# A hybrid decoder layer on one core: the FFN norm's factors in the gate and up weights, sums in order of use, rows two tiles ahead

## The chip, the cores and the metric

The kernel runs on one core of one Trainium2 chip. Its time is the device time of one execution in microseconds (us); the figure compared is the median over runs. One core has TensorE (PE; its weight loads are listed apart as PEld), VectorE (DVE), ScalarE (ACT), GpSimd (POOL) and SyncE (SP), which here issues nearly all DMAs. Each engine works through its own instructions in a fixed order and waits on semaphores for the others.

## The reference

One decoder layer on `x` of 1024 rows and 1024 columns, all in float32. What matters here is its second half:

```python
x = x + rmsnorm(m @ w_out[i], mix_post_norm[i])
h = rmsnorm(x, ffn_pre_norm[i])
f = (jax.nn.silu(h @ w_gate[i]) * (h @ w_up[i])) @ w_down[i]
x = x + rmsnorm(f, ffn_post_norm[i])
...
def rmsnorm(x, g):
    y = xf * lax.rsqrt(jnp.mean(xf * xf, axis=-1, keepdims=True) + EPS)
    return (y * g.astype(jnp.float32)).astype(x.dtype)
```

`m` holds the normalised outputs of an attention group and of a convolution group, 512 columns each. The FFN is 2816 wide (`w_gate` and `w_up` are 1024 x 2816).

## The kernel before

**Arithmetic.** TensorE multiplies in a rounded form (fp32r). To keep float32 accuracy, `split` makes of each value a high half (a cast on ScalarE, L196) and a low half (a subtraction, L197, on VectorE in the stretch of interest); a product is then three matmuls: high by high, high by low, low by high.

**Stages.** Attention and convolution come first. The output projection is done in two halves: `wo_c` handles the convolution's columns and stores its result to `y_d`; `wo_a(t)`, for the eight row tiles t of 128 rows, loads that result and the rows of `x`, adds the attention's half (24 wide matmuls; L1003 adds the bank to `y`), takes the mean square (L217 on ScalarE), the power -0.5 (L213 on VectorE, L214 on GpSimd), multiplies by `mix_post_norm` (L1009), adds the rows of `x` (L1010; on GpSimd for the tiles in `XP`, that is 2, 4 and 6, else on VectorE), stores the new `x`, takes the mean square again, and makes the normalised row `n1` in one VectorE instruction that multiplies by the row's factor and by `ffn_pre_norm`, broadcast over partitions (L1016). `h2_turn(t)` transposes `n1` (L1037, eight transposes), copies the banks (L1039 for tiles 0 to 3, which are stored to `hr_d` at L1047; L1041 for 4 to 7, which stay) and splits them into `B11`, `B21`, `B22`.

**The FFN** is a seven-product scheme for a two-by-two block product (Strassen's, in Winograd's form). Two blocks of 128 FFN columns form a pair `fp`; there are 11 pairs, each with `m` = 0 (gate) and 1 (up). Products run in the order `ORDER`, (1, 2, 6, 5, 7, 3, 4), each of 12 wide matmuls (128x128 by 128x512; L1122, L1124, L1125). Its left operand comes from the weights: `raw_load(fp, i)` loads two raw tiles of 128x1024 (L1079), `factor(fp, m, p)` makes sums of their halves on GpSimd (L1092, L1093, L1098, L1101) and splits them. Its right operand is a block of the activations for products 1, 2, 3 and a block sum for 6, 5, 7, 4, called `T2`, `T1`, `T3`, `T4`. The sums of 128x2048 elements are L1205 and L1206 on VectorE and L1207 and L1215 on GpSimd. A product's bank is evacuated by a ScalarE copy (L1134) or a VectorE addition (L1140 and its neighbours L1138 and L1144); silu is L1142. `s_factors` stores sums of the result to `sc_d`, `w_factors` those of `w_down` to `wc_d`, for the down products (L1280 to L1282), which follow.

**What sets the order.** The source's order is an input to a scheduler at build time, which fixes each engine's instruction order. So the order on an engine can differ from the source's. Memory is managed by hand: `mf(n)` takes the least recently freed n units of 128x512 float32 (30 units in all), `mr(n)` those in fp32r (72 units), and a transfer into a buffer waits for the last reader of what lay there. The main loop over `seq` writes a factor five products ahead of its use (`AHEAD`).

Of the kernel before, what the change touches and what calls it, by code (L numbers as in the profile page):

```python
# [15 lines left out]
P = 128  # L16
# [116 lines left out]
def hybrid_layer(ctx: ExitStack, tc: tile.TileContext, x, x_t, p_t, cols_in, positions,  # L133
                 w_in, w_conv, q_norm, kv_norm, w_uq, w_ukv, w_out, mix_post_norm, ffn_pre_norm, w_gate, w_up, w_down, ffn_post_norm,
# [91 lines left out]
    rows = mem_rows.a[0:28, 0:P]  # L226
# [174 lines left out]
    wcol = cols(28)  # L401

    def columns():
# [3 lines left out]
        pe.transpose(b[:, 32:60], rows, ident[0:28, 0:28])  # L407
        dve.tensor_copy(posc, b[:, 0:T])
        dve.tensor_copy(wcol, b[:, 32:60])
# [584 lines left out]
    g_mix, g_ffn = mf(2, MG), mf(2, MG)  # L994
    brow(mix_post_norm, D, g_mix)
    brow(ffn_pre_norm, D, g_ffn)

    def wo_a(t):
        xr, y = mf(2, ML), mf(2, ML)
        sp.dma_start(xr.a, x[t * P : (t + 1) * P, :])  # L1000
        sp.dma_start(y.a, y_d[t * P : (t + 1) * P, :])
# [8 lines left out]
        (pool if t in XP else dve).tensor_tensor(y.a, y.a, xr.a, op=ALU.add)  # L1010
# [5 lines left out]
        dve.scalar_tensor_tensor(n1.a, y.a, r, g_ffn.a, op0=ALU.mult, op1=ALU.mult)  # L1016
# [63 lines left out]

    def factor(fp, m, p):
        a = raws[fp, m, 0].a
# [5 lines left out]
        else:  # L1088
            b = raws[fp, m, 1].a
            a21, a22 = b[:, 0:U], b[:, U:]  # L1090
            if p == 6:
                pool.tensor_tensor(a21, a21, a22, op=ALU.add)  # L1092
                pool.tensor_tensor(a11, a21, a11, op=ALU.subtract)  # L1093
                src = a11
            elif p == 5:
                src = a21
            elif p == 7:
                pool.tensor_tensor(a21, a22, a11, op=ALU.subtract)  # L1098
                src = a21
            elif p == 3:  # L1100
                pool.tensor_tensor(a12, a12, a11, op=ALU.subtract)  # L1101
                src = a12
            else:
                src = a22
# [73 lines left out]

    raw_load(0, 0, MW)
    for p in (1, 2):  # L1180
        for m in range(2):
            factor(0, m, p)
    tr[0], tr[1] = mf(4, ((22, 26),)), mf(4, ((26, 30),))
    for t in range(T):
        wo_a(t)
        if t > 0:
            h2_turn(t - 1)
    for d in (mTa, wo):
        for h, l in d.values():
            free(h, l)  # L1190
    free(g_mix, g_ffn)
    head = [(0, m, p) for p in (1, 2) for m in range(2)]
    raw_load(1, 0, MW)
    for i in head[:2]:
        product(*i)
    h2_turn(T - 1)
    b11 = mf(4, MG)
    sp.dma_start(four(b11), hr_d[:, 0:4, :])
    for i in head[2:]:
        product(*i)  # L1200
    for p in (1, 2):
        for m in range(2):
            factor(1, m, p)
    b12, b22 = tr[0], tr[1]
    dve.tensor_tensor(b12.a, b22.a, b12.a, op=ALU.subtract)  # L1205
    dve.tensor_tensor(b11.a, b12.a, b11.a, op=ALU.add)  # L1206
    pool.tensor_tensor(b22.a, b22.a, b11.a, op=ALU.subtract)  # L1207
    for n, v in (("T2", b11), ("T1", b22), ("T3", b12)):
        h, l = tf[n] = pair(4, BT)
        split(h.a, l.a, v.a)  # L1210
        if n != "T2":
            free(v)
# [3 lines left out]
    h, l = tf["T4"] = pair(4, BT)  # L1216
    split(h.a, l.a, b21.a)
    free(b11, b21)
    for p in (1, 2):
        for m in range(2):  # L1220
            product(1, m, p)
    raw_load(0, 1)
# [4 lines left out]
    for i in range(-AHEAD, len(seq)):  # L1227
        if i + AHEAD < len(seq):
            fp, m, p = seq[i + AHEAD]
            if p == 6 and m == 0:  # L1230
                if fp > 0:
                    raw_load(fp, 1)
            factor(fp, m, p)
            if p == 7 and m == 1 and 1 < fp + 1 < NP:
                raw_load(fp + 1, 0)
        if i >= 0:
            fp, m, p = seq[i]
            product(fp, m, p)
            if p == 5 and m == 1:
                w_factors(fp)  # L1240
            if p == ORDER[-1] and m == 1:
                s_factors(fp)
# [142 lines left out]
    for t in range(T - 3, T):  # L1385
# [4 lines left out]
        "w_ukv", "w_out", "mix_post_norm", "ffn_pre_norm", "w_gate", "w_up", "w_down",  # L1390
# [42 lines left out]
```

## Time and profile before

| | us |
|---|---|
| median of 3 runs | 1263.94 (1262.7 to 1264.12) |
| the profiled execution | 1265.35 |
| its span in the trace | 1263.6 |

Times in the views are counted from the start of the span. The page gives each engine's busy time, and in 40 slices its busy share in tenths. The views of the trace used below are: windows (busy time of each engine in a stretch), groups of instructions (by line and shape: count, busy time, mean duration in ns, idle time before and its releasers), TensorE's waits (who was waited for: us in total, times, longest) and the chain that ended last (start, length, what). An instruction is named by its line in the kernel, so L1003 is the addition in `wo_a`.

### The profile page before, as it was taken

How to read it: one execution, taken by the hardware profiler on the slowest of the kernel's cores; microseconds unless marked ns; L12 is line 12 of the kernel's file. 1: busy time of each engine (PE TensorE's matmuls, PEld its weight loads, DVE VectorE, ACT ScalarE, POOL GpSimd, SP SyncE). 2: the span in 40 equal slices, each digit the busy share in tenths (PEclk: the TensorE clock that was granted, in tenths of full speed). 3: DMA queues.
4: the chain of work that ended last, by engine and by line, in shares of the span. 5: the costliest groups of instructions: out<-in, count | busy, mean ns of one | idle time of the engine just before them, and what ended most of it. 6: DMA issues, size and time to landing. Idle time of an engine off the chain costs nothing.

```text
span 1263.6 us, 16523 instructions
## 1 busy us (share of the span) xinstructions
PE 1214.1 (96%) x5950; PEld 1024.2 (81%) x5950; DVE 775.4 (61%) x1114; ACT 558.0 (44%) x1011; POOL 494.5 (39%) x372
## 2 busy tenths in 40 slices
PE   7999999999999997759999999999999999999998
PEld 6898888888999886548888888888887888888886
DVE  7945457388867576687564564756547554566632
ACT  6543323277766744543333343333335445454220
POOL 5523545236634222287965665766611000000100
PEclk9999999999999999879999999999999999999999
DMA  6422554994541746435644445544349766665331
GB/s 244 169 67 99 192 184 152 287 343 113 136 104 57 285 164 203 158 110 190 230 160 142 144 157 183 175 167 147 137 126 327 239 194 190 196 217 169 105 112 50
DMA packets 87789, 215.67 MB, mean 171 GB/s; under 512 B 8791, under 2 KB 17275, under 8 KB 86395
## 3 DMA queue, kind: packets, MB, share of 16 engines
q1 hardware_dynamic: 87648, 214.60, 51.3%
q8 instruction: 46, 0.75, 0.3%
q14 instruction: 37, 0.30, 0.1%
q10 hardware_dynamic: 58, 0.02, 0.0%
HBM read 143.28 MB, written 71.04 MB: 170 GB/s over the span
## 4 chain that ended last, share of the span: by engine, by line
PE 79%; DVE 8%; DMA 8%; ACT 2%; issue 2%; POOL 2%; SPq 0%; DVEq 0%; ACTq 0%; POOLq 0%
PE banks L1124 10%; PE banks L1125 10%; PE banks L1122 10%; PE banks L207 7%; PE banks L208 7%; PE banks L209 7%; PE banks L1280 5%; PE banks L1281 5%; PE banks L1282 5%; DVE mem_r L197 4%; PE banks L842 2%; DMA mem_f<-y_d 2%; PE banks L813 1%; PE banks L809 1%; PE banks L814 1%
## 5 line engine op out<-in xcount | busy, mean ns | idle before, releaser
L197 DVE TENSOR_TENSOR mem_r<-mem_f,mem_r 128x512 fp32r<-128x512 f32 (+2 forms) x353 | 345.7, 1005 | 215.0 <-ACT mem_r L196 203.5
L196 ACT CAST mem_r<-mem_f 128x512 fp32r<-128x512 f32 (+3 forms) x356 | 234.7, 686 | 389.8 <-PE banks L1124 159.5
L1122 PE MATMUL banks<-mem_r 128*128 128x512 f32 x616 | 243.8, 396 | 10.9 <-DVE mem_f L1003 7.0
L1124 PE MATMUL banks<-mem_r 128*128 128x512 f32 x616 | 243.8, 396 | 10.1 <-DVE mem_r L197 10.1
L207 PE MATMUL banks<-mem_r 128*128 128x512 f32 (+2 forms) x664 | 247.1, 377 | 4.0 <-DVE mem_f L1003 3.3
L208 PE MATMUL banks<-mem_r 128*128 128x512 f32 (+2 forms) x664 | 247.4, 373 | 1.9 <-POOL mem_r L197 1.9
L209 PE MATMUL banks<-mem_r 128*128 128x512 f32 (+2 forms) x664 | 246.6, 373 | 0.0
L1125 PE MATMUL banks<-mem_r 128*128 128x512 f32 x616 | 243.0, 395 | 0.0
L214 POOL TENSOR_TENSOR small<-small,mhalf 128x1 f32<-128x1 f32 (+2 forms) x42 | 34.7, 828 | 318.2 <-DVE small L213 315.6
L1122 PEld LDWEIGHTS banks<-mem_r 128*128 128x128 f32 x616 | 117.8, 191 | 37.1 <-issue 7.4
L1124 PEld LDWEIGHTS banks<-mem_r 128*128 128x128 f32 x616 | 118.1, 192 | 35.4 <-DVE mem_r L197 11.0
L207 PEld LDWEIGHTS banks<-mem_r 128*128 128x128 f32 x664 | 126.0, 191 | 25.6 <-DVE mem_f L1003 3.8
L208 PEld LDWEIGHTS banks<-mem_r 128*128 128x128 f32 x664 | 126.5, 190 | 22.5 <-POOL mem_r L197 2.1
L209 PEld LDWEIGHTS banks<-mem_r 128*128 128x128 f32 x664 | 126.4, 190 | 21.0
L1125 PEld LDWEIGHTS banks<-mem_r 128*128 128x128 f32 x616 | 118.0, 192 | 25.0
L1280 PE MATMUL banks<-mem_r 128*128 128x512 f32 x308 | 119.1, 390 | 1.6 <-ACT mem_r L196 1.6
L1281 PE MATMUL banks<-mem_r 128*128 128x512 f32 x308 | 119.8, 389 | 0.0
L1282 PE MATMUL banks<-mem_r 128*128 128x512 f32 x308 | 118.8, 389 | 0.0
L827 POOL TENSOR_TENSOR mem_f<-mem_f,stats 128x640 f32<-128x640 f32 (+5 forms) x64 | 72.6, 1148 | 92.3 <-DVE stats L826 46.5
L197 DVE TENSOR_TENSOR mem_r<-banks,mem_r 128x512 fp32r<-128x512 f32 (+3 forms) x134 | 79.8, 621 | 14.5 <-ACT mem_r L196 13.6
L1140 DVE TENSOR_TENSOR mem_f<-banks,mem_f 128x512 f32<-128x512 f32 x66 | 45.3, 688 | 68.2 <-PE banks L1125 68.1
L196 ACT CAST mem_r<-banks 128x512 fp32r<-128x512 f32 (+3 forms) x134 | 67.3, 545 | 27.0 <-PE banks L842 13.6
(172 smaller groups left out, 1644.7 us busy)
## 6 DMA issues: line engine op xcount, KB each, us to landing
sc_d<-mem_f SPq DMA_DIRECT2D x77, 256.0 KB, 3.1
mem_f<-sc_d SPq DMA_DIRECT2D x77, 256.0 KB, 2.7
mem_f<-in_w_up_dram SPq DMA_DIRECT2D x22, 512.0 KB, 4.2
mem_f<-in_w_gate_dram SPq DMA_DIRECT2D x22, 512.0 KB, 4.6
mem_f<-in_w_down_dram SPq DMA_DIRECT2D x22, 512.0 KB, 4.5
wc_d<-mem_f SPq DMA_DIRECT2D x22, 512.0 KB, 3.0
mem_f<-wc_d SPq DMA_DIRECT2D x44, 256.0 KB, 3.0
mem_f<-in_w_down_dram SPq DMA_DIRECT2D x33, 256.0 KB, 3.3
```

Source lines behind the costliest of these rows:

```text
L196: act.copy(h, src)
L197: (eng or dve).tensor_tensor(l, src, h.bitcast(F32), op=ALU.subtract)
L207: pe.matmul(o, wh, vh, start=i == 0, stop=False)
L208: pe.matmul(o, wh, vl, start=False, stop=False)
L209: pe.matmul(o, wl, vh, start=False, stop=i == n - 1)
L827: pool.tensor_tensor(pt.a[:, 0:n], pt.a[:, 0:n], sm.to_broadcast([P, n]), op=ALU.mult)
L1122: pe.matmul(b, wh.a[:, c], th[:, k], start=first and k == 0, stop=False, skip_group_check=True)
L1124: pe.matmul(b, wh.a[:, c], tl[:, k], start=False, stop=False, skip_group_check=True)
L1125: pe.matmul(b, wl.a[:, c], th[:, k], start=False, stop=k == 3, skip_group_check=True)
L1280: pe.matmul(b, ah.a[:, c], bh.a, start=first, stop=False, skip_group_check=True)
L1281: pe.matmul(b, ah.a[:, c], bl.a, start=False, stop=False, skip_group_check=True)
L1282: pe.matmul(b, al.a[:, c], bh.a, start=False, stop=last, skip_group_check=True)
```

## The change

Six edits:

1. `ffn_pre_norm` is no longer broadcast to a row tile. Its 1024 values come in as eight more columns (`wcol`, 28 to 36), 128 values along the partitions in each. `raw_gain` multiplies the raw weights by them in place, eight `act.mul` of 128x128 on each raw tile (L1090), called from `factor` for p = 1 and p = 6. The row keeps only its own factor, applied by `act.mul` of 128x1024 on ScalarE (L1021 in the new file) where L1016 was on VectorE.
2. The rows of `x` and `y` are loaded by `wo_rows`, called two tiles ahead, `y` first.
3. `XP` is gone: the addition of `x` is on VectorE for all tiles.
4. `factor` runs its sums for pair 0 on VectorE.
5. The block sums L1207 and L1215 move from GpSimd to VectorE (L1237, L1246), and sums, splits, factors and products are written in order of use.
6. `raw_load(fp + 1, 1)` is written behind the last factor of pair fp instead of ahead of product 6 of pair fp + 1, and the four head products are written ahead of the last turn.

```diff
-    g_mix, g_ffn = mf(2, MG), mf(2, MG)
+    g_mix = mf(2, MG)
     brow(mix_post_norm, D, g_mix)
-    brow(ffn_pre_norm, D, g_ffn)
+    xy = {}
+    def wo_rows(t):
+        xr, y = xy[t] = mf(2, ML), mf(2, ML)
+        sp.dma_start(y.a, y_d[t * P : (t + 1) * P, :])
+        sp.dma_start(xr.a, x[t * P : (t + 1) * P, :])
     def wo_a(t):
...
-        (pool if t in XP else dve).tensor_tensor(y.a, y.a, xr.a, op=ALU.add)
+        dve.tensor_tensor(y.a, y.a, xr.a, op=ALU.add)
...
-        dve.scalar_tensor_tensor(n1.a, y.a, r, g_ffn.a, op0=ALU.mult, op1=ALU.mult)
+        act.mul(n1.a, y.a, r)
...
+    def raw_gain(fp, m, i):
+        r = raws[fp, m, i].a
+        for k in range(KD):
+            c = slice(k * P, (k + 1) * P)
+            act.mul(r[:, c], r[:, c], wcol[:, 28 + k : 29 + k])
     def factor(fp, m, p):
+        eng = pool if fp else dve
+        if p in (1, 6):
+            raw_gain(fp, m, int(p == 6))
...
+    wo_rows(0)
+    wo_rows(1)
     raw_load(0, 0, MW)
-    for p in (1, 2):
-        for m in range(2):
-            factor(0, m, p)
     for t in range(T):
+        if t + 2 < T:
+            wo_rows(t + 2)
         wo_a(t)
         if t > 0:
             h2_turn(t - 1)
+        if t == T // 2:
+            for p in (1, 2):
+                for m in range(2):
+                    factor(0, m, p)
...
-    for p in (1, 2):
-        for m in range(2):
-            factor(1, m, p)
     dve.tensor_tensor(b12.a, b22.a, b12.a, op=ALU.subtract)
+    both(factor, 1, 1)
+    both(product, 1, 1)
     dve.tensor_tensor(b11.a, b12.a, b11.a, op=ALU.add)
-    pool.tensor_tensor(b22.a, b22.a, b11.a, op=ALU.subtract)
+    t_split("T2", b11)
+    both(factor, 1, 2)
+    both(product, 1, 2)
+    both(factor, 0, 6)
+    dve.tensor_tensor(b22.a, b22.a, b11.a, op=ALU.subtract)
+    t_split("T1", b22)
...
-    pool.tensor_tensor(b21.a, b21.a, b11.a, op=ALU.subtract)
+    both(factor, 0, 5)
+    t_split("T3", b12)
+    factor(0, 0, 7)
+    dve.tensor_tensor(b21.a, b21.a, b11.a, op=ALU.subtract)
+    t_split("T4", b21)
...
-    for i in range(-AHEAD, len(seq)):
+    for i in range(len(seq)):
...
-            if p == 6 and m == 0:
-                if fp > 0:
-                    raw_load(fp, 1)
             factor(fp, m, p)
+            if p == ORDER[-1] and m == 1 and fp + 1 < NP:
+                raw_load(fp + 1, 1)
```

Each place below is a run of one engine's instructions in its order, as line, operation, output and input, and shape, with a count where equal ones follow one another. The first is ScalarE's, at the start of the tile loop. L946 evacuates the projection's first half, L196 casts, L217 is the mean square. Before:

```order
L946 ACTIVATE mem_f<-banks,small 128x512 x3
L196 CAST mem_r<-mem_f 128x512 x3
L946 ACTIVATE mem_f<-banks,small 128x512 x2
L217 ACTIVATE mem_f,small<-mem_f 128x1024 x5
L1039 COPY mem_f<-banks 128x512
```

And now:

```order
L946 ACTIVATE mem_f<-banks,small 128x512 x2
L1090 ACTIVATE mem_f<-mem_f,small 128x128 x8
L196 CAST mem_r<-mem_f 128x512
L946 ACTIVATE mem_f<-banks,small 128x512
L196 CAST mem_r<-mem_f 128x512
L946 ACTIVATE mem_f<-banks,small 128x512 x2
L1090 ACTIVATE mem_f<-mem_f,small 128x128 x8
L196 CAST mem_r<-mem_f 128x512 x2
L217 ACTIVATE mem_f,small<-mem_f 128x1024 x2
L1021 ACTIVATE mem_f<-mem_f,small 128x1024
```

The gains of pair 0's two first raw tiles (L1090) stand between the last evacuations of `wo_c` and the first mean square, though the source writes them behind tile 4.

The second place is ScalarE's at the end of the tile loop, in front of the last tile's turn. L1134 evacuates a product's bank and L1142 is silu with the load of its table. Before:

```order
L1134 COPY mem_f<-banks 128x512 x2
L196 CAST mem_r<-mem_f 128x512 x4
L1142 ACT_TABLE_LOAD
L1142 ACTIVATE mem_f<-mem_f 128x512
L1041 COPY mem_f<-banks 128x4x128 x2
L196 CAST mem_r<-banks 128x4x128
L217 ACTIVATE mem_f,small<-mem_f 128x1024
L1134 COPY mem_f<-banks 128x512
```

And now, where L1156 is that silu:

```order
L217 ACTIVATE mem_f,small<-mem_f 128x1024
L1090 ACTIVATE mem_f<-mem_f,small 128x128 x8
L1021 ACTIVATE mem_f<-mem_f,small 128x1024
L217 ACTIVATE mem_f,small<-mem_f 128x1024
L1090 ACTIVATE mem_f<-mem_f,small 128x128 x8
L1156 ACT_TABLE_LOAD
L1156 ACTIVATE mem_f<-mem_f 128x512
L196 CAST mem_r<-mem_f 128x512
L1021 ACTIVATE mem_f<-mem_f,small 128x1024
L1090 ACTIVATE mem_f<-mem_f,small 128x128 x8
```

Three sets of gains now lie around the last rows' multiplication L1021, two of them ahead of it, with the table load between.

The third place is VectorE's behind the last turn. L1205 is the first block sum, L1206 the second, L1140 an evacuation, L197 a low half. Before:

```order
L1205 TENSOR_TENSOR mem_f<-mem_f 128x2048
L197 TENSOR_TENSOR mem_r<-banks,mem_r 128x4x128
L1206 TENSOR_TENSOR mem_f<-mem_f 128x2048
L1140 TENSOR_TENSOR mem_f<-banks,mem_f 128x512
L197 TENSOR_TENSOR mem_r<-mem_f,mem_r 128x2048
```

And now, where L1229, L1232 and L1237 are the sums, L1154 an evacuation, and L1106 and L1107 factors of pair 0:

```order
L1229 TENSOR_TENSOR mem_f<-mem_f 128x2048
L197 TENSOR_TENSOR mem_r<-banks,mem_r 128x4x128
L197 TENSOR_TENSOR mem_r<-mem_f,mem_r 128x512 x2
L1232 TENSOR_TENSOR mem_f<-mem_f 128x2048
L1106 TENSOR_TENSOR mem_f<-mem_f 128x512
L197 TENSOR_TENSOR mem_r<-mem_f,mem_r 128x2048
L1154 TENSOR_TENSOR mem_f<-banks,mem_f 128x512
L1237 TENSOR_TENSOR mem_f<-mem_f 128x2048
L1107 TENSOR_TENSOR mem_f<-mem_f 128x512
L197 TENSOR_TENSOR mem_r<-mem_f,mem_r 128x2048
```

VectorE now holds the third sum (L1237) and the factors of pair 0 (L1106, L1107), which GpSimd had.

More of the change, by code (lines that the diff above doesn't have):

```diff
@@ L400, in hybrid_layer @@
     posc = cols(T)
-    wcol = cols(28)
+    wcol = cols(36)
     def columns():
@@ L406, in columns @@
         pe.transpose(b[:, 0:T], prow, ident[0:T, 0:T])
-        pe.transpose(b[:, 32:60], rows, ident[0:28, 0:28])
+        pe.transpose(b[:, 32:68], rows, ident[0:36, 0:36])
         dve.tensor_copy(posc, b[:, 0:T])
-        dve.tensor_copy(wcol, b[:, 32:60])
+        dve.tensor_copy(wcol, b[:, 32:68])
         ps.put(ids)
```

65 lines of the change are left out of this document (29 added, 36 removed).

## The prediction

> **What bounds the kernel now.** I read the page's first sections, then the stretch where TensorE has gaps, and there waits, groups and the chain.
>
> ```profile
> span 1263.6 us, 16523 instructions
> PE 1214.1 (96%) x5950; PEld 1024.2 (81%) x5950; DVE 775.4 (61%) x1114; ACT 558.0 (44%) x1011; POOL 494.5 (39%) x372
> PE   7999999999999997759999999999999999999998
> PEclk9999999999999999879999999999999999999999
> ...
> PE 79%; DVE 8%; DMA 8%; ACT 2%; issue 2%; POOL 2%; SPq 0%; DVEq 0%; ACTq 0%; POOLq 0%
> ```
>
> TensorE is busy for 96% of the span. Apart from the two ends, slices 16 to 18 (474 to 569 us) are its weak ones (7, 7, 5), with a lower clock in 17 and 18. They hold most of the row-tile loop and the sums behind it, where all parts of the change but one act. The windows below are, in order, the loop up to the turn of tile 7; from there until TensorE runs densely; and the loop over the pairs. Columns: busy us of PE, PEld, DVE, ACT, POOL with instruction counts, granted clock, DMA share, GB/s.
>
> ```profile
> 442.20:528.20 86.00, 71.42 (x320) 57.54 (x318) 55.39 (x70) 38.99 (x71) 22.03 (x23) 0.94 0.53 175
> 528.20:568.00 39.80, 26.10 (x89) 19.81 (x90) 36.67 (x20) 16.82 (x21) 28.36 (x12) 0.74 0.35 124
> 568.00:941.00 373.00, 373.00 (x1647) 308.98 (x1646) 218.45 (x237) 136.51 (x236) 241.40 (x161) 1.00 0.48 163
> ```
>
> The third row gives the price of a wide matmul at full clock: 373.00 / 1647 = 0.2265 us, with no gap. Against it I price the first two. The groups of TensorE there and its waits:
>
> ```profile
> L207 PE MATMUL banks<-mem_r 128*128 128x512 f32 x63 | 24.8, 394 | 3.3 <-DVE mem_f L1003 3.3
> L1122 PE MATMUL banks<-mem_r 128*128 128x512 f32 x51 | 24.2, 477 | 10.9 <-DVE mem_f L1003 7.0 <-ACT mem_r L196 3.4 <-ACT mem_f L1041 0.5
> L1037 PE MATMUL banks<-ident,mem_f 128*128 128x128 f32 x64 | 8.4, 274 | 4.1 <-DVE mem_f L1016 2.7 <-DVE small L213 1.4
> PE banks L1124 <- DVE mem_r L197: 10.1, 2, 5.5
> 518.79 0.89 PE banks L1037 x8
> ```
>
> L207's group and its two sisters are 189 matmuls of the output projection, L1122's and its sisters 153 of the FFN products, and eight transposes of one tile take 0.89 us. Work of the first window, all of the projection, seven turns and 72 product matmuls: 261 x 0.2265 + 7 x 0.89 = 65.3; **lost** 86.0 - 65.3 = 20.7 us. Second: 81 x 0.2265 + 0.89 = 19.2; lost 39.8 - 19.2 = 20.6 us. So 41.3 us is all there is to win here. The waits name what ends last: evacuations of the tile loop (L1003) first, then the low halves of splits on VectorE (L197: 10.1 us in two waits). The remainder is the halved clock behind gaps.
>
> **The change, part by part.**
>
> *(b) Behind the turn of tile 7.* Before, VectorE does sums and splits while GpSimd does two sums and four factors.
>
> ```profile
> L197 DVE TENSOR_TENSOR mem_r<-mem_f,mem_r 128x2048 fp32r<-128x2048 f32 x4 | 17.7, 4423 | 0.0
> L197 DVE TENSOR_TENSOR mem_r<-mem_f,mem_r 128x512 fp32r<-128x512 f32 x10 | 11.6, 1193 | 2.6 <-ACT mem_r L196 2.6
> L1205 DVE TENSOR_TENSOR mem_f<-mem_f 128x2048 f32<-128x2048 f32 x1 | 2.3, 2293 | 0.2 <-ACT mem_f L1041 0.2
> L1140 DVE TENSOR_TENSOR mem_f<-banks,mem_f 128x512 f32<-128x512 f32 x2 | 1.4, 680 | 0.0
> L1207 POOL TENSOR_TENSOR mem_f<-mem_f 128x2048 f32<-128x2048 f32 x1 | 5.0, 4953 | 0.0
> L196 ACT CAST mem_r<-mem_f 128x512 fp32r<-128x512 f32 x308 | 182.9, 620 | 312.1 <-PE banks L1124 159.5 <-PE banks L1281 75.6 <-POOL mem_f L1098 25.4
> ```
>
> The same elements take 2.29 us on VectorE (L1205) and 4.42 beside GpSimd (L197); so a big split costs 2.1 us more in company. In the new order GpSimd has no large work here; the factors of pair 0 and both block sums it held stand on VectorE. Until the last operand that holds TensorE (T1) VectorE has six big and eleven small instructions: 6 x 2.29 + 11 x 0.68 = 21.2 us. Ahead of them ScalarE has eight gains (2.2, below) and six copies and casts of 0.62: 5.9. With 1 us for the halved clock, TensorE is dense 28.1 us behind the turn, in which it does 64 product matmuls and eight transposes (15.4 us), since 48 instead of 72 come before the turn. Lost 12.7 against 20.6: **-7.9 us**. Cover that might go: were GpSimd busy here still, six big ones at 4.42 would add 12.8 and the part would lose 5.
>
> *Gains on ScalarE.* 44 raw weight tiles get eight 128x128 multiplications each, 352 instructions in place. The trace has none of that shape. The nearest rows, and one piece of ScalarE's timeline (start, length):
>
> ```profile
> L580 ACT ACTIVATE mem_f<-mem_f,small 128x1024 f32<-128x1024 f32 x4 | 4.6, 1154 | 5.9 <-POOL mem_f L573 5.9
> L485 ACT ACTIVATE mem_f<-banks,small 128x256 f32<-128x256 f32 x8 | 3.8, 476 | 3.2 <-DVE small L387 2.1 <-PE banks L209 1.0
> L487 ACT ACTIVATE mem_f<-banks,small 128x32 f32<-128x32 f32 x8 | 2.3, 292 | 0.0
> 442.56 1.26 ACT L946 ACTIVATE mem_f<-banks,small 128x512 f32<-128x512 f32 x2
> L946 ACT ACTIVATE mem_f<-banks,small 128x512 f32<-128x512 f32 x16 | 10.8, 688 | 7.7 <-PE banks L209 7.4
> ```
>
> Between 32 elements (0.292 us) and 256 (0.476), 128 come to 0.37; two L946 in a row take 1.26, not 1.38, so neighbours overlap by 0.11. Eight cost 8 x 0.37 - 7 x 0.11 = 2.2 us, which I take, since it lies between both rows; with 0.292 and 0.476 for one it would be 1.6 and 3.0, the ends. All use the same engine, though only L580 reads the tile from SBUF. 44 x 2.2 = 97 us more for ScalarE, which has 136.5 of 373 us in the pair loop: cover is ample on the average, at nothing in the sum if in time. About four sets lie on the path of (a) and (b), so the ends move the sum by -2.4 and +3.2 us.
>
> The Trainium skill ("ScalarE: Activation LUTs", What ACT_TABLE_LOAD costs) gives 186 ns + 0.833 ns per element, about 93 ns for a pointer operand, and 93 ns overlap. A tile's eight would be an estimated 2.4 us by that page, and the sum 0.8 us more than by my term.
>
> *(a) The tile loop up to the turn of tile 7.* What moves: L1016 (1.30 us of VectorE) becomes a ScalarE multiplication (L1021; 1.15 by L580's row); three additions go from GpSimd (2.41) to VectorE (1.22); rows load two tiles ahead; the gains of pair 0 are hoisted.
>
> ```profile
> 435.87 5.62 DMA mem_f<-in_w_gate_dram
> 447.76 1.29 DVE mem_f L1003
> 449.14 1.16 ACT mem_f L217 x2
> 455.79 1.30 DVE mem_f L1016
> 464.49 3.54 DMA hr_d<-mem_f
> 468.94 7.70 DMA mem_f<-y_d
> 479.59 5.86 DMA mem_f<-y_d
> 488.15 2.41 POOL mem_f L1010
> 497.06 1.22 DVE mem_f L1010
> 509.22 1.29 DVE mem_f L1003
> L1142 ACT ACT_TABLE_LOAD x1 | 1.3, 1283 | 0.0
> ```
>
> I re-timed the order step by step with these durations, each wait on what it needs. Although the source writes the first factors behind tile 4, the order has 16 gains ahead of the first square (L217). The gate tile's delay the projection's evacuations on ScalarE, hence the store that frees the up tile's buffer; that lands near 451.6, and eight gains and two casts later the first square runs at 454.9, not 449.1: 5.8 us late. Second, loads "two tiles ahead" wait on SyncE: from tile 4 on, y takes the buffer that the hr store four tiles earlier leaves. With the turn of tile 3 at 494.6: 0.9 transposes, 1.2 copies, 3.5 store, 5.9 load gives L1007 of tile 7 at 506.1 (before, L1003 at 509.2). So the late start is made up by shorter steps. Third, pair 1's up tile is issued behind the turn of tile 5 (509.9) and lands 4.6 later; then ScalarE has, in front of the last row's multiplication, gains 2.1, multiplication 1.2, square 1.2, gains 2.1, table 1.3, silu and cast 1.2, and the multiplication itself 1.15: 524.7, plus 2 for y loads as slow as the rows above: turn at 526.7. TensorE has done 237 x 0.2265 + 7 x 0.89 = 59.9 of the 84.5 us from 442.2: lost 24.6 against 20.7, **+3.9 us**. What is late next is no longer VectorE's multiplication but the raw load in ScalarE's queue.
>
> *(c) The pair loop.* TensorE waits for nothing there now. Added on the path: gains between each load and GpSimd's factor, and in ScalarE's queue evacuations stand behind them. SyncE issues the second raw tiles at the end of the preceding pair, but into buffers the sum stores free.
>
> ```profile
> mem_f<-in_w_gate_dram SPq DMA_DIRECT2D x22, 512.0 KB, 4.6
> sc_d<-mem_f SPq DMA_DIRECT2D x77, 256.0 KB, 3.1
> wc_d<-mem_f SPq DMA_DIRECT2D x22, 512.0 KB, 3.0
> L1101 POOL TENSOR_TENSOR mem_f<-mem_f 128x512 f32<-128x512 f32 x22 | 35.5, 1614 | 14.7 <-DVE mem_r L197 14.1
> ```
>
> The tightest pair by the order: store 3.1, load 4.6, gains 2.2, four GpSimd factors 6.5, store 3.0, load 4.6, eight gains and four of the next tile 3.3, evacuation and cast 0.6 each, low half 1.2: 29.7 us, against 133 matmuls = 30.1 in which TensorE has other work. Slack 0.4; the next tightest that I followed has 4.6. At these medians **0**.
>
> Smaller parts at nothing: the lost broadcast load lies before the loop, eight more columns make one transpose wider, and AHEAD's prologue only reorders writing.
>
> Sum: +3.9 - 7.9 + 0 = -4.0. The profiled execution took 1265.35 us (1263.6 span), 1.4 over the median of 1263.94; it becomes 1261.4, the median **1260.0**.
>
> **The rivals.**
>
> *No gain* (**1264**): y loads at 5.9 to 7.7 throughout, or ScalarE's queue, give back the 4 us. For: the chain's y rows; the change then does not load early, as buffers decide. Against: VectorE's relief is independent of it. 20%.
>
> *Slower* (**1270**): one mechanism, in the pair loop: a gain at the head of ScalarE's queue waits for its load, and behind it stand evacuations which free TensorE's banks. It decides from transfers 3% longer than their medians (0.4 of 15.3 us). At half as long again (a y row, 512 KB like a weight tile, took 7.70, 1.7 times 4.6) 7.7 us come late: 7.3 lost in the tightest pair, 3.1 in the next: 1260.0 + 10. For: the slack. Against: ScalarE is 37% busy there, and medians hold already under a DMA share of 0.48. 24%. Beside this stands a rule of the Trainium skill ("ScalarE: Activation LUTs", Rules for kernel authors): multiplications go to VectorE, not ScalarE.
>
> *More* (**1255**): the tile loop is not later, since the up tile lands early and a set of gains costs 1.6: (b) alone with 1 us more, -9. 14%.
>
> **How the numbers follow.** Forecast 42%: its own range is 1256 to 1264 (the gains' ends, and a us or so for the loads). The range 1252 to 1270 takes in the rivals and leaves out the tails. A measurement of this kernel tells about 0.2% (2.5 us) from no change. Faster: the forecast below 1261.4 (0.30) and "more" (0.14): 0.44. Same: the rest of the forecast (0.12) and most of "no gain" (0.18): 0.30. Slower: 0.24 and 0.02 from "no gain": 0.26.
>
> **What would show it.** (b) is right if L197's 128x2048 group has a mean near 2.3 and VectorE's wait before L1138 falls from 10.1. (a) is right if the first square comes near 455 and the last turn near 527, the table load following a gain. (c) is right if the windows of the pair loop have TensorE at its full width; a wait of L1136 for ScalarE beyond 1 us in that stretch makes the slower rival true. A 128x128 gain under 0.15 or over 0.4 us makes me wrong on its price; a first square near 449 on the hoisting.

## The result, and the profile after

The changed kernel takes 1275.65 us (median of 4 runs, 1272.08 to 1278.92); the kernel before, run beside it, 1264.03. The ratio is 1.0095 with an interval from 1.0079 to 1.0112: slower by 11.6 us, where 1260.0 was forecast, and outside the range. The profiled execution took 1278.92, at the upper end of its runs.

The page of the changed kernel, with the rows that answer to those shown of before:

```profile
span 1276.9 us, 16861 instructions
PE 1220.1 (96%) x5950; PEld 1022.9 (80%) x5950; DVE 772.4 (60%) x1119; ACT 662.2 (52%) x1371; POOL 464.4 (36%) x359
PE   7899999999999997799899989999999999999998
PEclk9999999999999998789999999999999999999999
...
PE 63%; DMA 12%; DVE 9%; ACT 7%; POOL 6%; issue 3%; SPq 0%; POOLq 0%; ACTq 0%; DVEq 0%
```

ScalarE's share has grown by 104 us of work. TensorE's slices 16 to 18, weak before (7, 7, 5), are 7, 7, 9, so the part behind the last turn is better; but two slices further on, 20 and 24, both in the pair loop, have fallen to 8. The chain, 79% TensorE before, now has 12% DMA and 7% ScalarE. The windows put numbers to it: the tile loop up to the last turn, from there to 568 us, and a stretch of the pair loop; the last row is the same stretch of the kernel before.

```profile
442.44:524.66 82.22, 66.96 (x296) 53.37 (x295) 45.56 (x64) 50.46 (x97) 13.14 (x17) 0.91 0.55 183
524.66:568.00 43.34, 37.96 (x145) 30.04 (x146) 34.55 (x34) 28.68 (x55) 8.79 (x5) 0.85 0.33 112
570.00:900.00 330.00, 317.93 (x1381) 258.84 (x1380) 199.87 (x201) 191.04 (x480) 209.00 (x139) 0.99 0.47 158
```

```profile
570.00:900.00 330.00, 330.00 (x1457) 273.36 (x1456) 197.16 (x209) 120.50 (x209) 221.53 (x148) 1.00 0.49 169
```

In the third row TensorE has started 1381 matmuls in 330 us; at 0.2265 us each that is 312.8 us of work, so 17.2 us are lost. Before there were 1457: nothing lost. This number, 330.0 less the count times 0.2265, is called the *loop loss* below (a few records missing from a trace can shift it by a us). Over the whole loop, from 570 to 963.6, the same count gives 19.2 us. Its waits in the changed kernel, over the whole span:

```profile
PE banks L1136 <- ACT mem_f L1148: 13.5, 13, 3.3
PE banks L1042 <- ACT mem_f L1021: 8.2, 3, 5.8
...
PE banks L1136 <- ACT mem_r L196: 5.3, 3, 4.0
```

The first row is new: a product's first matmul waits for a bank until ScalarE's copy (L1148) has emptied it, thirteen times, 13.5 us, all in the pair loop. The longest, 3.3 us, ended at 754.9. ScalarE's timeline around it (start, length, instruction, and in brackets the idle time before it and its releaser):

```profile
743.54 0.58 ACT L1148 COPY mem_f<-banks 128x512 f32<-128x512 f32 x1
749.52 2.45 ACT L1090 ACTIVATE mem_f<-mem_f,small 128x128 f32<-128x128 f32 x8 [5.39 <-DMA mem_f<-in_w_gate_dram]
752.57 0.40 ACT L1090 ACTIVATE mem_f<-mem_f,small 128x128 f32<-128x128 f32 x1 [0.59 <-DMA mem_f<-in_w_up_dram]
752.88 0.60 ACT L196 CAST mem_r<-mem_f 128x512 fp32r<-128x512 f32 x1
753.38 0.98 ACT L1090 ACTIVATE mem_f<-mem_f,small 128x128 f32<-128x128 f32 x3
754.27 0.56 ACT L1148 COPY mem_f<-banks 128x512 f32<-128x512 f32 x1
```

ScalarE stood idle for 5.39 us for the gate tile, then worked through twelve gains, and only then copied out the bank. What made that tile late stands in the timelines of ScalarE, GpSimd and SyncE ahead of it:

```profile
733.72 2.45 ACT L1090 ACTIVATE mem_f<-mem_f,small 128x128 f32<-128x128 f32 x8 [5.64 <-DMA mem_f<-in_w_gate_dram]
736.25 1.30 POOL L1106 TENSOR_TENSOR mem_f<-mem_f 128x512 f32<-128x512 f32 x1 [4.64 <-ACT mem_f L1090]
...
744.31 1.74 POOL L1186 TENSOR_TENSOR mem_f<-mem_f 128x512 f32<-128x512 f32 x1
746.08 0.33 SPq L1084 DMA_DIRECT2D mem_f<-in_w_gate_dram  x1
```

GpSimd waited 4.64 us for the gains of the gate tile before, then worked without a break through three factors and three sums of `w_factors`. The last of these (L1186) was the last reader of the buffer that the late gate tile was to take, and SyncE issued the load when it had ended. The chain of waits goes on with the up tile behind it:

```profile
744.83 3.48 DVE mem_r L197 x2
748.30 0.02 issue
748.32 0.33 SPq L1084
...
748.75 5.04 DMA wc_d<-mem_f
753.78 0.02 issue
753.80 3.42 DMA mem_f<-in_w_up_dram
...
757.30 1.27 ACT mem_f L1090 x4
```

This up tile waits for a store out of the buffer that it is to take, lands 3.4 us after that, and the gains follow at once. A load waits for a buffer, a gain for the load, and releases of buffers stand behind the gain.

### The profile page after: what moved, and what is told of

The parts are those of the page before. It is cut to its first block, busy times and chain, and to the rows that moved or that the text cites. A ratio compares the mean times of both kernels' runs of the same rounds, so it can differ in the third digit from the quotient of the medians.

```text
span 1276.9 us, 16861 instructions
## 1 busy us (share of the span) xinstructions
PE 1220.1 (96%) x5950; PEld 1022.9 (80%) x5950; DVE 772.4 (60%) x1119; ACT 662.2 (52%) x1371; POOL 464.4 (36%) x359
## 4 chain that ended last, share of the span: by engine, by line
PE 63%; DMA 12%; DVE 9%; ACT 7%; POOL 6%; issue 3%; SPq 0%; POOLq 0%; ACTq 0%; DVEq 0%
PE banks L207 9%; PE banks L209 9%; PE banks L208 9%; PE banks L1304 5%; PE banks L1305 5%; PE banks L1306 5%; PE banks L1136 4%; DVE mem_r L197 4%; PE banks L1138 4%; PE banks L1139 4%; ACT mem_f L1090 3%; PE banks L842 2%; DMA wc_d<-mem_f 2%; DMA mem_f<-in_w_down_dram 2%; DMA mem_f<-in_w_up_dram 2%
## 5 line engine op out<-in xcount | busy, mean ns | idle before, releaser
L197 DVE TENSOR_TENSOR mem_r<-mem_f,mem_r 128x512 fp32r<-128x512 f32 (+2 forms) x353 | 342.9, 998 | 259.9 <-ACT mem_r L196 243.9
L196 ACT CAST mem_r<-mem_f 128x512 fp32r<-128x512 f32 (+3 forms) x356 | 233.6, 683 | 253.9 <-PE banks L1305 77.3
L1136 PE MATMUL banks<-mem_r 128*128 128x512 f32 x616 | 245.3, 399 | 21.4 <-ACT mem_f L1148 13.5
L1136 PEld LDWEIGHTS banks<-mem_r 128*128 128x128 f32 x616 | 117.7, 191 | 53.1 <-ACT mem_f L1148 19.3
L214 POOL TENSOR_TENSOR small<-small,mhalf 128x1 f32<-128x1 f32 (+2 forms) x42 | 37.5, 894 | 334.9 <-DVE small L213 332.4
L1090 ACT ACTIVATE mem_f<-mem_f,small 128x128 f32<-128x128 f32 x352 | 109.2, 391 | 81.5 <-DMA mem_f<-in_w_gate_dram 48.0
L197 DVE TENSOR_TENSOR mem_r<-banks,mem_r 128x512 fp32r<-128x512 f32 (+3 forms) x134 | 79.7, 620 | 10.9 <-ACT mem_r L196 10.1
L196 ACT CAST mem_r<-banks 128x512 fp32r<-128x512 f32 (+3 forms) x134 | 67.3, 545 | 26.8 <-PE banks L842 13.6
```

The costliest lines, as they stand in the source:

```text
L196: act.copy(h, src)
L197: (eng or dve).tensor_tensor(l, src, h.bitcast(F32), op=ALU.subtract)
L1090: act.mul(r[:, c], r[:, c], wcol[:, 28 + k : 29 + k])
L1136: pe.matmul(b, wh.a[:, c], th[:, k], start=first and k == 0, stop=False, skip_group_check=True)
```

## The experiments

All ran beside runs of the kernel before on the same chip, whose medians lay between 1262.98 and 1264.12. "Loop loss" is from the window 570 to 900 of each profile. It comes from one execution each, and executions of one kernel spread by several us: the traced one of the changed kernel is at the upper end of its runs, those of dve_evac, pool_gain, before_gains and buf_p3 are at the lower end of theirs. Differences of some 3 us between loop losses say little.

| kernel | median, us | ratio to before, interval | loop loss, us |
|---|---|---|---|
| changed kernel | 1275.65 | 1.0079 to 1.0112 | 17.2 |
| no_gain | 1251.24 | 0.9889 to 0.9922 | 0.9 |
| work_no_wait | 1273.16 | 1.0064 to 1.0094 | 17.9 |
| wait_no_work | 1254.05 | 0.9916 to 0.9945 | 3.2 |
| work_at_evac | 1250.08 | 0.9871 to 0.9901 | 0.0 |
| half_gain | 1270.27 | 1.0034 to 1.0071 | 13.4 |
| dve_evac | 1273.13 | 1.0060 to 1.0094 | 10.6 |
| pool_gain | 1269.34 | 1.0031 to 1.0063 | 13.4 |
| before_gains | 1275.88 | 1.0069 to 1.0119 | 5.7 |
| old_loads | 1273.09 | 1.0064 to 1.0097 | 13.6 |
| sep_buf | 1291.65 | 1.0200 to 1.0250 | 26.0 |
| buf_down | 1286.95 | 1.0161 to 1.0210 | 14.7 |
| buf_p3 | 1275.57 | 1.0069 to 1.0122 | 11.5 |
| buf_p5 | 1278.26 | 1.0092 to 1.0132 | 13.6 |
| turn_gain | 1252.79 | 0.9906 to 0.9935 | 0.0 |
| turn_gain_pool | 1258.38 | 0.9943 to 0.9973 | 1.1 |
| turn_gain_rows0 | 1259.95 | 0.9953 to 0.9979 | 4.1 |

### Are the gains the cause?

**no_gain:**

```diff
-        if p in (1, 6):
-            raw_gain(fp, m, int(p == 6))
```

> The changed kernel without the 352 gains on the raw weights; ffn_pre_norm is left out of the computation. Three theories. W (wait): a gain at the head of ScalarE's queue waits for its raw tile, and the evacuations behind it hold TensorE's banks. L (length): the 94 us of extra ScalarE work in the pair loop by itself makes evacuations late. S (sequence): the new place of the raw loads and the rewritten order of factors starve TensorE, with or without gains. W and L: the 13.5 us of waits for L1148 and the slow clock behind them go, TensorE loses under 2 us between 568 and the last product (19 us in the changed kernel), and the time is 1253 to 1257 us. S: the waits stay, 1270 to 1276 us.

1251.24 us, below the expected 1253: the gains cost 24.4 us, and all the rest of the change gains 12.1 against the 1263.32 of the kernel before in that group. The sequence (S) cannot starve TensorE by itself: the loop loss is 0.9. Not all of the gains' price lies in the pair loop: in the traces TensorE starts its 300th product matmul 9.2 us earlier without gains (585.6 against 594.8), and the last one 27.6 us earlier, so 18.4 are of the loop and a third comes ahead of it.

### The length, the wait, or both?

**work_no_wait** and **wait_no_work** were to separate them.

```diff
+        if not i:
+            return
-        r = raws[fp, m, i].a
-        for k in range(KD):
-            c = slice(k * P, (k + 1) * P)
-            act.mul(r[:, c], r[:, c], wcol[:, 28 + k : 29 + k])
+        r = raws[fp, m, 0].a
+        for k in range(2 * KD):
+            act.mul(junk[:], r[:, 0:P], wcol[:, 28 + k % KD : 29 + k % KD])
```

> The changed kernel with the same 352 multiplications of 128x128 on ScalarE, but sixteen at a time at product 6's factor, reading the first raw tile of the pair, which has long landed, and writing to a tile of their own; ffn_pre_norm is left out of the computation. W: ScalarE is as busy as in the changed kernel (about 660 us) but waits for no load, so the time is within 3 us of the version without gains, 1254 to 1259 us. L: evacuations are as late as in the changed kernel, 1268 us or more.

```diff
-        for k in range(KD):
-            c = slice(k * P, (k + 1) * P)
-            act.mul(r[:, c], r[:, c], wcol[:, 28 + k : 29 + k])
+        act.mul(r[:, 0:32], r[:, 0:32], wcol[:, 28:29])
```

> The changed kernel with one multiplication of 128x32 on each raw tile in place of eight of 128x128: ScalarE waits for the same loads at about the same places, but works some 13 us instead of 109; ffn_pre_norm is left out of the computation but for 32 columns of each tile. W: most of the waits of TensorE for L1148 stay, each shorter by the up to 2.4 us of work behind the landing: 4 to 10 us of waits in the pair loop, 1261 to 1269 us. L: within 2 us of the version without gains, 1253 to 1257 us.

Taken at their word, both speak for L: 1273.16 with work, 1254.05 with the wait alone. But the first is no clean test. ScalarE's group of those multiplications, in the window 570 to 945, shows that they did wait for loads:

```profile
L1092 ACT ACTIVATE junk<-mem_f,small 128x128 f32<-128x128 f32 x284 | 113.8, 401 | 60.6 <-DMA mem_f<-in_w_gate_dram 54.3
```

60.6 us idle before them, 54.3 of it for the gate tiles: the scheduler put them right behind the first tile's landing. The second is clean, and tells against W as it stood: its one small multiplication waits longer than the gains do (window 570 to 900; below it the changed kernel's group in the same window), and TensorE loses 3.2 us.

```profile
L1088 ACT ACTIVATE mem_f<-mem_f,small 128x32 f32<-128x32 f32 x34 | 10.9, 321 | 93.9 <-DMA mem_f<-in_w_gate_dram 47.8 <-DMA mem_f<-in_w_up_dram 44.0 <-issue 1.6
```

```profile
L1090 ACT ACTIVATE mem_f<-mem_f,small 128x128 f32<-128x128 f32 x280 | 86.7, 391 | 57.9 <-DMA mem_f<-in_w_gate_dram 34.1 <-DMA mem_f<-in_w_up_dram 16.5 <-issue 3.7
```

93.9 us of idle time at the head of ScalarE's queue can cost 3 us; 57.9 can cost 17. So length alone was tried again, at a place with no load in front.

**work_at_evac:**

```diff
-        if p in (1, 6):
-            raw_gain(fp, m, int(p == 6))
...
             act.copy(o, b)
+            for k in range(4 if p == 5 else 5):
+                act.mul(junk[:], o[:, 0:P], wcol[:, 28 + k : 29 + k])
         elif p == 4 and m == 0:
             act.activation(o, b, AF.Silu)
+            for k in range(4):
+                act.mul(junk[:], o[:, 0:P], wcol[:, 28 + k : 29 + k])
```

> The changed kernel with the gains' 352 multiplications of 128x128 moved: four or five behind each evacuation by ScalarE, reading what that evacuation has just written and writing to a tile of their own, so that none waits for a load; ffn_pre_norm is left out of the computation. The earlier try at this still waited for loads (60.6 us of ScalarE's idle time in the pair loop lay before those multiplications). Theories now: W (wait and length together at one place: a gain waits for its tile and the evacuation stands behind it), L (length alone: ScalarE's extra 94 us, wherever they stand), C (cycle: longer work between a raw tile's landing and its buffer's release makes the next loads later). W and C: within 3 us of the version without gains, 1250 to 1255 us. L: 1262 us or more.

1250.08 us, no loop loss, with ScalarE busier than in the changed kernel (its window: 220.4 of 330 us against 191.0):

```profile
570.00:900.00 330.00, 330.00 (x1457) 273.26 (x1456) 202.32 (x214) 220.41 (x490) 222.44 (x149) 1.00 0.48 170
```

L falls. The same 352 multiplications are free there and cost 24 us between a raw tile's landing and its use.

**half_gain** asks how the loss grows with the length at that place.

```diff
-        for k in range(KD):
-            c = slice(k * P, (k + 1) * P)
+        for k in range(0, KD, 2):
+            c = slice(k * P, (k + 2) * P)
```

> The changed kernel with four multiplications of 128x256 on each raw tile in place of eight of 128x128, so some 1.5 us a tile in place of 2.45, waiting for the same loads; every other block of 128 columns of the weights gets its neighbour's factors, so ffn_pre_norm is half left out. If the loss in the pair loop grows evenly with the length on the chain (2.0 us at one multiplication of 0.32 us, 19.0 at 2.45): about 11 to 12 us lost, 1264 to 1269 us. If there is slack first and the loss sets in behind it: under 8 us lost, 1258 to 1264 us.

1270.27 us and a loop loss of 13.4: above both expectations (the even one ended at 1269). One multiplication of 128x256 took 498 ns in the window 570 to 930, so a tile's four take some 1.7 us, against 2.45 and, in wait_no_work, 0.32. Loop loss over length: 0.9 at none, 3.2 at 0.32, 13.4 at some 1.7, 17.2 at 2.45. Most of the loss is there at 1.7 us already. No run lies between 0.32 and 1.7, so a slack of some tenths of a us is neither shown nor excluded.

### ScalarE's queue, or the raw tile's path?

**dve_evac** takes the evacuations out of ScalarE's queue:

```diff
         if p in (1, 6, 5):
-            act.copy(o, b)
+            dve.tensor_copy(o, b)
```

> The changed kernel, gains and all, with the copies of the products' banks (L1148 there) on VectorE instead of ScalarE; the whole computation is done. W: the evacuations no longer stand behind gains, the waits of TensorE for L1148 (13.5 us) go, and the pair loop loses under 6 us instead of 19: 1256 to 1263 us. C: raw loads are as late as before, TensorE waits for operands instead, and the pair loop loses 12 us or more: 1267 to 1276 us.

The loop loss falls from 17.2 to 10.6, between both; the time, 1273.13, is C's. Evacuations behind gains are a part of the loss; more than half is left when they are gone, and 6.0 us of what is left are waits for the same copies, now on VectorE.

**pool_gain** takes the gains out of ScalarE's queue, at much the same length (2131 ns a tile):

```diff
-        for k in range(KD):
-            c = slice(k * P, (k + 1) * P)
-            act.mul(r[:, c], r[:, c], wcol[:, 28 + k : 29 + k])
+        pool.tensor_tensor(bank3(r, KD), bank3(r, KD), wcol[:, 28:36].unsqueeze(2).to_broadcast([P, KD, P]), op=ALU.mult)
```

> The changed kernel with the gains on GpSimd, one multiplication of 128x1024 by a broadcast of the eight columns on each raw tile (some 2.4 us, as long as ScalarE's eight) in place of 352 on ScalarE; the whole computation is done. W (ScalarE's queue is what counts): evacuations and casts no longer stand behind gains, TensorE loses under 5 us between 570 and 900: 1252 to 1260 us. C (the cycle is as long as before, and GpSimd is in it): TensorE loses 12 us or more there, and waits for operands: 1266 to 1285 us.

1269.34 us, loop loss 13.4: C's side. GpSimd is busy 293 of 330 us there, so a part of it may be GpSimd's own load; the run does not separate that.

That loads themselves come later, and not only what waits for them, is read from SyncE's timeline against TensorE's. Without gains, the last pair's second gate tile is issued with 322 product matmuls still to run, with the short multiplication of wait_no_work 317, in the changed kernel 294: 28 x 0.2265 = 6.3 us later by TensorE's own progress. The gain delays the next load too.

### Which buffer, which order?

**sep_buf** keeps the down weights' buffers (w_factors) apart, as both raw loads above waited for a reader of theirs, a GpSimd sum or a store.

```diff
-        w = [mf(2), mf(2)]
+        w = [mf(2, ((26, 30),)), mf(2, ((26, 30),))]
```

(All other buffers of the pair loop then come from units 0 to 26.)

> The changed kernel, gains and all, with the buffers of the down weights' sums (w_factors) kept apart: 4 units for them alone, 26 for the raw tiles and the products' blocks, so that a raw load no longer waits for a store of w_factors; the whole computation is done. C (cycle: gain, GpSimd's factors, w_factors' sums behind them, their store, the next raw load, the next gain) is cut there: TensorE loses under 6 us between 570 and 900 instead of 17, 1257 to 1266 us. If the loads are late for another reason, the loss stays over 12 us: 1270 to 1277 us.

The opposite of C's number: 1291.65 us, loop loss 26.0. Cutting that link alone does not help. But the run also leaves the raw tiles and blocks four units fewer, which may make loads later by itself; it does not separate the two.

**before_gains** puts the gains alone into the kernel before.

```diff
     def factor(fp, m, p):
+        if p in (1, 6):
+            raw_gain(fp, m, int(p == 6))
...
-        dve.scalar_tensor_tensor(n1.a, y.a, r, g_ffn.a, op0=ALU.mult, op1=ALU.mult)
+        act.mul(n1.a, y.a, r)
```

> The kernel before with the first edit alone: the gains on the raw weights and the row's factor by ScalarE, all else in the old order, with the rows loaded in their own step, sums on GpSimd, the raw loads at their old place. If the gains cost by themselves what they cost in the changed kernel (19 us in the pair loop, 5 in the tile loop): 1280 to 1292 us. Rival: the new place of the raw loads is half of it: 1268 to 1276 us.

1275.88 us, the rival's side: 12.3 us above its group's 1263.62, but with a loop loss of only 5.7. The stretch before takes none of it in the traces: by 570 us this kernel has started 168 product matmuls, the kernel before 161. Behind the loop its trace is 3.0 us longer, most of it one wait of 2.6 for a cast; the rest stays unplaced, as the traced execution is 2.6 us below its median. So the gains' price in the pair loop seems to depend on the order around them.

**old_loads** puts the second raw tiles' loads back to their old place in the changed kernel.

```diff
+            if p == 6 and m == 0:
+                raw_load(fp, 1)
             factor(fp, m, p)
-            if p == ORDER[-1] and m == 1 and fp + 1 < NP:
-                raw_load(fp + 1, 1)
```

> The changed kernel, gains and all, with the second raw tiles of a pair written where the kernel before has them, ahead of product 6's factor of that pair, instead of at the end of the preceding pair; the whole computation is done. The kernel before with gains alone lost 5.9 us between 570 and 930, the changed kernel 19.0. If the new place of those loads is what turns the gains' length into waits (their buffers are taken earlier and ScalarE's order has the gains earlier, at the head of its queue): 4 to 9 us lost there and 1260 to 1267 us. If it is the rest of the new order: 15 us or more lost, 1271 to 1277 us.

1273.09 us, loop loss 13.6: between both numbers, nearer to the second; the time lies in the second range. The place of the loads is a small part, if it is one.

**buf_down, buf_p3, buf_p5** change only which free buffers come first, once, at the start of the pair loop:

```diff
+    for u in reversed(range(FU)):
+        if not mf.live[u]:
+            mf.clock += 1
+            mf.freed[u] = mf.clock
     seq = [(fp, m, p) for fp in range(NP) for p in ORDER for m in range(2)
```

(In the other two, the units come in pairs in a random order.)

> The changed kernel, gains and all, in which the free buffers of the float32 memory are put in descending order once, at the start of the pair loop, so that the raw loads get other buffers with other last readers; same instructions, whole computation. Chain of buffer releases: the loss of TensorE between 570 and 930 (19.0 us in the changed kernel) differs from it by over 3 us in at least one of the three kernels with other buffers. Rival (the number of instructions and ScalarE's queue set it, whatever the buffers): all three within 2 us of 19.0, 1273 to 1278 us.

> As the preceding one with a random order of the free buffers, in pairs. Chain of buffer releases: loss differs by over 3 us from 19.0 in at least one of the three. Rival: within 2 us of it.

> As the preceding one with another random order of the free buffers. Chain of buffer releases: loss differs by over 3 us from 19.0 in at least one of the three. Rival: within 2 us of it.

Between 570 and 930 they lose, by the same count, 14.8, 11.4 and 13.7 us instead of 19.1, over 3 us off, as the chain of releases expects. But two of the times, 1275.57 and 1278.26, lie at the changed kernel's, whose own profiled execution was 3.3 us above its median, and buf_down, at 1286.95, has one wait of 11.7 us at the start of the loop (TensorE's waits, window 570 to 930; this one began at 561.3):

```profile
PE banks L1136 <- ACT mem_f L1148: 18.1, 8, 11.7
```

So the order of the buffers can add 11 us, and none of these orders takes the loss to the 5.7 of before_gains. What in the old order keeps it there is open.

### Without the weights' gains, and the two other steps

**turn_gain** applies the factors to the transposed rows, where they again lie along the partitions: eight multiplications of 128x128 a tile, 64 in all, in place of the 352 and of 16 copies.

```diff
-            if first:
-                act.copy(raw.a[:, q * U : (q + 1) * U], b)
-            else:
-                act.copy(four(tr[q])[:, :, o], bank3(b, 4))
+            d3 = bank3(raw.a[:, q * U : (q + 1) * U], 4) if first else four(tr[q])[:, :, o]
+            for j in range(4):
+                act.mul(d3[:, j], b[:, j * P : (j + 1) * P], wcol[:, 28 + 4 * q + j : 29 + 4 * q + j])
+            ps.put(ids)
             if first or q:
...
-                split(four(h)[:, :, o], four(l)[:, :, o], bank3(b, 4))
-            ps.put(ids)
+                split(four(h)[:, :, o], four(l)[:, :, o], d3)
...
-        if p in (1, 6):
-            raw_gain(fp, m, int(p == 6))
```

> The changed kernel with ffn_pre_norm applied to the transposed rows: each bank of four transposes is copied out by four multiplications of 128x128 with the gain (64 blocks in all per half of the tiles' eight, 64 in total), and the split reads the result; no gains on the weights. The whole computation is done. W and L: the pair loop has no waits, as without gains, and each turn of a row tile costs ScalarE about 1.5 us more; the tile loop hides most of it: 1254 to 1260 us, faster than the kernel before. S: 1270 us or more.

1252.79 us, ratio 0.9920 (0.9906 to 0.9935): faster than both kernels, by 10.5 and 22.9 us.

**turn_gain_pool** takes step (b) back in that version.

```diff
-        eng = pool if fp else dve
+        eng = pool
...
-    dve.tensor_tensor(b22.a, b22.a, b11.a, op=ALU.subtract)
+    pool.tensor_tensor(b22.a, b22.a, b11.a, op=ALU.subtract)
...
-    dve.tensor_tensor(b21.a, b21.a, b11.a, op=ALU.subtract)
+    pool.tensor_tensor(b21.a, b21.a, b11.a, op=ALU.subtract)
```

> The version with gains on the transposed rows, with two block sums and the factors of pair 0 back on GpSimd (part b undone). By the prediction's step (b), big splits on VectorE cost 4.4 us instead of 2.3 beside GpSimd and the stretch behind the last turn gets some 8 us longer: 1258 to 1263 us, and the 128x2048 splits there have a mean over 3.5 us. Rival: the order of use alone makes the gain, and the time stays within 2 us: 1251 to 1255 us.

1258.38 us, 5.6 more. VectorE's big splits, with GpSimd at work and, below, without (window 500 to 570 of turn_gain_pool and of turn_gain):

```profile
L197 DVE TENSOR_TENSOR mem_r<-mem_f,mem_r 128x2048 fp32r<-128x2048 f32 x4 | 14.9, 3750 | 1.4 <-ACT mem_r L196 1.4
```

```profile
L197 DVE TENSOR_TENSOR mem_r<-mem_f,mem_r 128x2048 fp32r<-128x2048 f32 x4 | 9.1, 2286 | 0.8 <-ACT mem_r L196 0.8
```

The same instruction takes 3.75 us in company and 2.29 alone. Step (b)'s mechanism holds; the order of use alone does not make the gain.

**turn_gain_rows0** loads the rows in their own step.

```diff
-    wo_rows(0)
-    wo_rows(1)
...
-        if t + 2 < T:
-            wo_rows(t + 2)
+        wo_rows(t)
         wo_a(t)
```

> The version with gains on the transposed rows, with the rows of x and y loaded in their own tile's step instead of two ahead. If buffers decide when the rows load, as the prediction's step (a) has it, the time stays within 2 us: 1251 to 1255 us. Rival: loading ahead is what shortens the tile loop: 1256 to 1261 us.

1259.95 us, 7.2 more: the rival's number, but not its mechanism. In the traces, 6.6 us apart, TensorE starts its 200th product matmul, behind the last turn, only 0.3 us later (565.5 against 565.2). By the end of the pair loop it is 4.3, far from the rows, and 2.3 more come behind the loop (other buffers, by the same reasoning as above, though no run shows it). So in these traces loading ahead does not shorten the tile loop.

## Why the prediction was wrong

**(a) The tile loop up to the last turn**: forecast 3.9 us worse. The window has 237 matmuls of the projection and products and seven turns, 59.9 us of work, in 82.22: lost 22.3 against 20.7, 1.6 worse. The mechanism was right to the point: first square forecast at 454.9, measured at 454.82; last turn forecast at 526.7 with 2 us of allowance, measured at 524.66. The hoisted gains and ScalarE's queue at the end of the loop are as described:

```profile
451.42 2.46 ACT L1090 ACTIVATE mem_f<-mem_f,small 128x128 f32<-128x128 f32 x8 [7.44 <-DMA mem_f<-in_w_up_dram]
453.78 1.13 ACT L196 CAST mem_r<-mem_f 128x512 fp32r<-128x512 f32 x2
454.82 1.05 ACT L217 ACTIVATE mem_f<-mem_f 128x1024 f32<-128x1024 f32 x1
...
523.46 1.15 ACT L1021 ACTIVATE mem_f<-mem_f,small 128x1024 f32<-128x1024 f32 x1
```

The reading that buffers decide when rows load is not refuted: turn_gain_rows0, with the rows loaded in their own step, is 0.3 us later behind the tile loop, and its 7.2 us arise elsewhere. The small net hides the gains' price ahead of the pair loop, 9.2 us in the trace of no_gain, which the rest of the change all but made up for.

**(b) Behind the last turn**: forecast 7.9 us better. The second window has 8 transposes and 137 matmuls, 31.9 us, in 43.34: lost 11.4 against 20.6, 9.2 better. The splits' mean is 2.28 us, as forecast near 2.3, and TensorE's wait for the low halves is gone from its list. Only the size was off, by 1.3 us.

**The gain's price**: 2.2 us a tile forecast, 2.45 measured. The page of the Trainium skill that was weighed ("ScalarE: Activation LUTs", What ACT_TABLE_LOAD costs) gave an estimated 2.4, and a single one took 391 ns, where its figures give an estimated 386. On the four sets of the sum that is 1 us.

**(c) The pair loop**: forecast 0, measured 19.2 us; this is the step that failed. The sentence was "Slack 0.4; the next tightest that I followed has 4.6. At these medians 0". Its chain was nearly the right one: load, gains, factors, store, load, gains, evacuation. In the round of the longest wait one term of it was too small: GpSimd's part took 9.8 us (736.25 to 746.05) where the sum has 6.5, since three of `w_factors`' sums stand among the factors; and the store's 3.0 were not waited for there. Above all, the chain was priced once, as a detour that either fits or doesn't. It comes back through the loop: a load that comes late makes the next load late, since its gain delays the release of buffers (6.3 us behind TensorE's progress by the last pair). With a slack of 0.4 us out of 30 and landings that spread from 3.4 (issued at 753.80) to 5.4 us (issued at 728.21), medians say little. The loss over the length of the gain, from 3.2 at 0.32 us to 17.2 at 2.45, is that of a path with little slack or none. The reason given for no cost, that ScalarE is at 37% there and has cover on the average, was no argument: work_at_evac has ScalarE at 67% of the window and loses nothing.

Together the three parts, 1.6 - 9.2 + 19.2, are 11.6 of the 13.3 us by which the spans of the two traces differ; 1.4 more lie behind the loop. That the medians differ by 11.6 too is chance.

**The slower rival** named this place and gave 1270, and its sign, a wait of L1136 for ScalarE beyond 1 us, came with 3.3. The runs bear out half of its mechanism: evacuations stand behind waiting gains (13.5 us of waits, and moving them off takes the loss from 17.2 to 10.6). Its price was short since it was worked out for two pairs, not for a loss that comes back through the loop (the thirteen waits ended between 594 and 910 us). The wait alone, which the rival put first, is nearly free: 3.2 us of loss. Of the rule that stood beside it (the Trainium skill, "ScalarE: Activation LUTs", Rules for kernel authors: multiplications to VectorE) no run can tell, as none has the gains on VectorE.

**What stays open**: how the loss divides between ScalarE's queue and the chain of buffers, since dve_evac and pool_gain each move load to an engine that matters; how much of the changed kernel's 17.2 is owed to its traced execution, 3.3 us above the median; and why gains cost 5.7 us in the old order's loop and 13.6 in the new one's with the loads at their old place.

## What to carry to other kernels

Work that is put between a load and its first use is not paid from an engine's idle share, but from the slack of that load's chain, up to the buffer that the next load waits for; if the chain comes round in every step of a loop, price it per round, and call a slack smaller than the spread of the landings none. Put a scaling where data passes anyway: the same factors cost 24.4 us on 44 weight tiles and 1.6 on the 16 banks of transposed rows. A change of several parts can hide a good one: without the gains, what was left gained 12 us.

## What was not expected of the hardware

A stop of TensorE cost more than the wait, but mostly not by its clock. In the window 570 to 900 of the changed kernel twelve waits of 0.2 to 3.3 us add up to 12.1 us, and 17.2 are lost. Two things make up 4.9 of the difference.

At each of the twelve, 0.27 us are lost beside the wait, 3.3 in all. The last matmul before it is recorded for its full 0.39 us (ends are modelled in the trace), where otherwise the next one starts after 0.2265; and the first one behind it holds the next one off for 0.11 us more.

The granted clock fell behind one wait only, the longest: to 0.53 in the 3.6 us from 755.69, where matmuls start up to 0.43 us apart, 1.6 us lost. Behind the wait of 1.7 us that ended at 627.6 it stayed at 1.00:

```profile
755.69:759.30 3.61, 3.61 (x10) 2.84 (x9) 2.56 (x3) 3.31 (x11) 2.89 (x2) 0.53 0.23 92
627.50:629.50 2.00, 1.90 (x8) 1.60 (x9) 1.67 (x2) 0.57 (x2) 2.00 (x2) 1.00 0.94 332
```
